# A pre-norm block pair with dense-evaluated expert layers: up-products of two experts interleaved, and pairs of heads and wider gate products in the second mixer

## The chip, the core and the metric

One core of a Trainium2 chip runs the whole program. The metric is the device time of one execution in microseconds. TensorE (PE) multiplies, its weight loads (PEld) run beside the multiplications; VectorE (DVE), ScalarE (ACT) and GpSimd (POOL) work on tiles, and SyncE (SP) issues most of the transfers.

## The reference

512 tokens of width 1024 pass through two blocks. The first mixes tokens with differential attention and retention, the second with a gated convolution and an mLSTM of eight heads; each is followed by the same kind of expert layer. What the change touches, cut to its core:

```python
# second mixer: i_pre, f_pre are 8 + 8 columns of the projection
proj = h @ w_in
ig = (i_pre + b_igate).transpose(0, 2, 1)
fg = (f_pre + b_fgate).transpose(0, 2, 1)
s_qk = einsum('bhtd,bhsd->bhts', qb, kb) * w_ts        # per head, d = 64
num = einsum('bhts,bhsv->bhtv', s_qk, vb) + ...        # v = 128

# expert layer: 128 * 128 = 16384 experts, 8 heads x 16 chosen per token
ub = take(u, eb);  z = einsum('thkd,td->thk', ub, hb)
a = gelu(z) * gb
out = einsum('thk,thkd->td', a, take(v, eb))
```

## The kernel before

All products that need fp32 accuracy are done as three in a rounded fp32 type: each operand is split into a high and a low part (ScalarE copies the high part, L86; VectorE subtracts for the low part, L87), and `mm3` (L99, its three matmuls are L101, L102 and L103) adds high x high, high x low and low x high into one PSUM accumulator.

The order is: first mixer (`mixer1`, L225), expert layer (`peer`, L447), second mixer (`mixer2`, L836), expert layer (`peer` again).

**The expert layer.** For three of the four token blocks (384 tokens) all 16384 experts are evaluated, in 128 groups of 128, each of which the code and this text call an expert e. `up(e)` (L495) loads a 128 x 1024 tile of weights through pool tag "w" (three buffers each of raw, high and low part), and issues 24 matmuls of 384 columns (8 blocks of the model width, three each) into a PSUM tile z of one bank, of which there are two; ScalarE applies gelu into a slot of a ring of 37 (L500). `down` (L681) multiplies the ring slot by the gate matrix wt (zero for experts that a token did not choose, VectorE L686), splits it into gh and gl, loads the expert's output weights through tag "v" (two buffers; expert 0 and part of the last ones use "w"), and issues 18 matmuls of 512 columns (L701) into six accumulators, three token blocks x two halves; consecutive matmuls go to the two halves in turn. wt is fetched for eight experts at a time from DRAM, where the router's work left it (L722). The first 36 up-products (LEAD) are done while the router still works; then the main loop (L725) goes on with one `up(e)` and one `down([e - 36])` per step, 92 steps with both. The last steps only have `down`, and the last two experts share one. The fourth token block's experts are gathered row by row (L708) and multiplied on VectorE (L711, L717) beside the main loop.

**The second mixer.** The normed input is written transposed, feature block by feature block, as fp32 (xf) and as split parts (L153 to L157). The 16 gate columns are computed in true fp32 with xf as the stationary operand: four token blocks x eight feature blocks of matmuls with 16 moving columns (L872), four copies (L873), eight transposes (L877) to get rows of the gates, two adds of the biases (L878). Then come the projections (L101 to L103 again), a chain on the gate rows (from L908), and a loop over the eight heads (L951): for each of four key blocks a decay row is fetched as a tile "we" (L957, four buffers), masked on GpSimd (L958) and exponentiated on ScalarE (L960); the scores of one head are an fp32 matmul over 64 rows (L962), VectorE multiplies both into "pw" (L965, six buffers); then ten matmuls of 129 columns per head give the weighted values (L973), which are normalised (L975 to L978).

A framework (tiles with pools) derives all waits from the buffers and orders each engine's instructions itself, so the order on an engine need not be that of the code.

## Time and profile before

| | us |
|---|---|
| median of three runs | 3453.27 (3444.09 to 3463.71) |
| profiled execution | 3443.86 |
| its span | 3442.0 |
| TensorE busy | 3328.5 (97%) |
| TensorE weight loads busy | 2889.2 (84%) |
| VectorE busy | 2496.2 (73%) |
| ScalarE busy | 1314.1 (38%) |
| GpSimd busy | 856.2 (25%) |

The mean granted clock of TensorE is 0.990 of full speed (full speed is 2.4 GHz, the other level 1.2 GHz). The profile gives busy time, and for each group of instructions what ended the idle time before it. A matmul's recorded duration is longer than its spacing, since matmuls overlap in the pipeline: the starts of neighbouring matmuls tell the rate. A matmul in true fp32 is recorded as two passes.

### The profile page before, as it was taken

To read this page: it belongs to the slowest core of one execution; us is meant where nothing else is said; L and a number is where in the kernel's file an instruction comes from. 1 tells how busy PE (TensorE), PEld (TensorE's weight loads), DVE (VectorE), ACT (ScalarE), POOL (GpSimd) and SP (SyncE) were. 2 spreads that over 40 slices of the span, in tenths; PEclk is the share of its full clock that TensorE was granted. 3 is DMA by queue.
4 is the path that set the end of the run, shared out by engine and by line. 5 is a ranking of instruction groups with operands and counts; after the bars stand their busy time and mean duration, and the time that the engine had idled before them with its cause. 6 is when DMAs were issued, how large, how long until landed. Compare 5 with 4: busy or idle time off the path is not lost. (4 is left out here: it accounts for less than half of the span.)

```text
span 3442.0 us, 46835 instructions
## 1 busy us (share of the span) xinstructions
PE 3328.5 (97%) x17462; PEld 2889.2 (84%) x17462; DVE 2496.2 (73%) x4641; ACT 1314.1 (38%) x1936; POOL 856.2 (25%) x732
## 2 busy tenths in 40 slices
PE   7989999899999999999999999899899999999998
PEld 6667889899999999777778888788899999999977
DVE  6765799777777787866565343779977777787785
ACT  4443345433333333334452223435533333333333
POOL 1000420144443444410000000240034444444420
PEclk9999999999999999999999999999999999999999
DMA  7212236799989888963437332325698899998883
GB/s 245 78 53 100 89 113 249 290 320 321 316 307 311 309 309 303 322 222 71 113 108 222 94 92 92 111 91 185 229 354 311 303 319 314 313 312 313 314 284 128
DMA packets 307396, 768.32 MB, mean 223 GB/s; under 512 B 22552, under 2 KB 123960, under 8 KB 300760
## 3 DMA queue, kind: packets, MB, share of 16 engines
q1 hardware_dynamic: 230832, 489.80, 42.6%
q0 software_dynamic: 76336, 275.53, 23.2%
q8 instruction: 136, 2.23, 0.3%
q14 instruction: 92, 0.75, 0.1%
HBM read 708.56 MB, written 56.69 MB: 222 GB/s over the span
## 5 line engine op out<-in xcount | busy, mean ns | idle before, releaser
L86 ACT ACTIVATE whi<-wraw 128x1024 fp32r<-128x1024 f32 x446 | 472.6, 1060 | 1109.8 <-PE z L102 547.8
L101 PE MATMUL z<-pxh,whi 128*128 128x384 f32 x2048 | 698.9, 341 | 3.8 <-ACT ga L500 2.5
L103 PE MATMUL z<-pxh,wlo 128*128 128x384 f32 x2048 | 695.5, 340 | 2.2 <-DVE wlo L87 2.2
L102 PE MATMUL z<-pxl,whi 128*128 128x384 f32 x2048 | 694.2, 339 | 0.8 <-DVE pxl L87 0.7
L87 DVE TENSOR_TENSOR wlo<-wraw,whi 128x1024 fp32r<-128x1024 f32 x398 | 485.1, 1220 | 284.5 <-ACT whi L86 284.3
L708 POOL DMA_INDIRECT row<-in_p_u,eidg x256 | 343.2, 1341 | 847.5 <-DVE row L711 466.4
L708 POOL DMA_INDIRECT row<-in_p_v,eidg x256 | 354.4, 1385 | 469.2 <-DVE yr L717 394.9
L717 DVE SCALAR_TENSOR_TENSOR yr<-row,gg,yr 128x1024 f32<-128x1024 f32 x254 | 325.8, 1283 | 144.5 <-DMA row<-in_p_v,eidg 141.7
L701 PE MATMUL acc<-vhi,gl 128*128 128x512 f32 x1308 | 406.2, 392 | 1.7 <-DVE gl L87 1.7
L701 PE MATMUL acc<-vhi,gh 128*128 128x512 f32 x1308 | 406.5, 392 | 0.1
L701 PE MATMUL acc<-vlo,gh 128*128 128x512 f32 x1308 | 405.3, 391 | 1.2 <-DVE vlo L87 1.2
L711 DVE SCALAR_TENSOR_TENSOR row<-row,pxr 128x1024 f32<-128x1024 f32 x256 | 309.0, 1222 | 122.3 <-DMA row<-in_p_u,eidg 121.4
L101 PEld LDWEIGHTS z<-pxh,whi 128*128 128x128 f32 x2048 | 384.8, 188 | 13.7 <-ACT ga L500 2.9
L102 PEld LDWEIGHTS z<-pxl,whi 128*128 128x128 f32 x2048 | 385.2, 188 | 11.9 <-DVE pxl L87 0.9
L103 PEld LDWEIGHTS z<-pxh,wlo 128*128 128x128 f32 x2048 | 384.8, 188 | 4.2 <-DVE wlo L87 3.9
L86 ACT ACTIVATE gh<-gw 128x384 fp32r<-128x384 f32 x256 | 134.5, 525 | 629.0 <-issue 383.1
L701 PEld LDWEIGHTS acc<-vlo,gh 128*128 128x128 f32 x1308 | 245.3, 188 | 56.3 <-DVE vlo L87 1.6
L701 PEld LDWEIGHTS acc<-vhi,gl 128*128 128x128 f32 x1308 | 245.2, 188 | 55.8 <-DVE gl L87 2.5
L701 PEld LDWEIGHTS acc<-vhi,gh 128*128 128x128 f32 x1308 | 243.7, 188 | 39.8 <-ACT gh L86 0.8
L87 DVE TENSOR_TENSOR vlo<-vraw,vhi 128x1024 fp32r<-128x1024 f32 x218 | 265.6, 1218 | 15.2 <-ACT vhi L86 15.2
L86 ACT ACTIVATE vhi<-vraw 128x1024 fp32r<-128x1024 f32 x218 | 230.7, 1058 | 42.0 <-DMA vraw<-in_p_v 34.1
L87 DVE TENSOR_TENSOR gl<-gw,gh 128x384 fp32r<-128x384 f32 x256 | 141.8, 554 | 136.2 <-ACT gh L86 135.7
(394 smaller groups left out, 5082.9 us busy)
## 6 DMA issues: line engine op xcount, KB each, us to landing
wraw<-in_p_uT SPq DMA_DIRECT2D x256, 512.0 KB, 5.6
vraw<-in_p_v SPq DMA_DIRECT2D x218, 512.0 KB, 5.7
wd<-wc SPq DMA_DIRECT2D x48, 1024.0 KB, 4.8
wt<-wd SPq DMA_DIRECT2D x32, 1536.0 KB, 13.0
wraw<-in_w_in SPq DMA_DIRECT2D x88, 512.0 KB, 4.6
adaw<-in_w_adaT SPq DMA_DIRECT2D x48, 512.0 KB, 4.5
wraw<-in_p_v SPq DMA_DIRECT2D x38, 512.0 KB, 5.3
wraw<-in_p_wq SPq DMA_DIRECT2D x32, 512.0 KB, 3.4
```

Of the source, the lines that this page charges most:

```text
L86: nc.scalar.activation(hi, src, AF.Copy)
L87: return (eng or nc.vector).tensor_tensor(lo, src, hi.bitcast(F32), op=ALU.subtract)
L101: mm(ps, lh, rh, start=start, stop=False)
L102: mm(ps, lh, rl, start=False, stop=False)
L103: mm(ps, ll, rh, start=False, stop=stop)
L701: nc.tensor.matmul(acc[j][n], gx[:, ts_], vx[:, n * 512:(n + 1) * 512], start=e == 0 and vx is vh and gx is gh, stop=e == P - 1 and gx is gl)
L708: nc.gpsimd.indirect_dma_start(out=row, out_offset=None, in_=lay["v" if half else "u"], in_offset=bass.IndirectOffsetOnAxis(ap=eidg[:, s:s ...
L711: nc.vector.scalar_tensor_tensor(row, row, 1.0, xr, op0=ALU.mult, op1=ALU.mult, accum_out=zg[:, s:s + 1])
L717: nc.vector.scalar_tensor_tensor(yr, row, gg[:, s:s + 1], yr, op0=ALU.mult, op1=ALU.add)
```

## The change

Three things. (1) A new `mm3s` issues the three products of `mm3` for several accumulators in turn, and a new `up2` uses it: the weights of two experts are loaded, and their 48 up-products alternate between the two z banks. The main loop calls it on every second step. (2) In the second mixer the gate columns become the stationary operand (16 columns) and xf the moving one (512 columns): eight matmuls into one 16 x 512 tile, one add of the bias, and two transfers to the two row tiles. (3) The scores of two heads, which lie in the two halves of the partitions, are issued in turn (`weighted`), with eight "pw" buffers for six; the value products follow for both heads.

```diff
--- before.py
+++ after.py
@@ -95,6 +95,13 @@
         nc.sync.dma_start(raw, view)
         self.last_split = self.split(hi, lo, raw, eng)
         return hi, lo
+
+    def mm3s(self, ops, start, stop):
+
+        mm = self.nc.tensor.matmul
+        for n in range(3):
+            for ps, lh, ll, rh, rl in ops:
+                mm(ps, ll if n == 2 else lh, rl if n == 1 else rh, start=start and n == 0, stop=stop and n == 2)
 
     def mm3(self, ps, lh, ll, rh, rl, start, stop):
         mm = self.nc.tensor.matmul
@@ -499,6 +506,15 @@
                 g.mm3(z, uh[:, k], ul[:, k], xh[:, k, S - TD:], xl[:, k, S - TD:], k == 0, k == KD - 1)
             nc.scalar.activation(ring[e % len(ring)], z, gelu)
 
+        def up2(e):
+
+            ws = [g.weights(lay["uT"][e + i], [P, KD, P]) for i in range(2)]
+            zs = [g.sb(zps, [P, TD], "z") for _ in range(2)]
+            for k in range(KD):
+                g.mm3s([(z, uh[:, k], ul[:, k], xh[:, k, S - TD:], xl[:, k, S - TD:]) for z, (uh, ul) in zip(zs, ws)], k == 0, k == KD - 1)
+            for i, z in enumerate(zs):
+                nc.scalar.activation(ring[(e + i) % len(ring)], z, gelu)
+
         def more(n, eng=None, keep=REST):
 
             nonlocal begun
@@ -723,8 +739,8 @@
             return wt
 
         for e in range(P + LEAD):
-            if begun <= e < P:
-                up(e)
+            if begun <= e < P and e % 2:
+                up2(e - 1)
             d = e - LEAD
             if d >= 0:
                 if d == 0:
@@ -848,9 +864,9 @@
         wcq = g.sb(sm, [P, 4, KD], "wcq")
         nc.gpsimd.dma_start(wca, a["conv_a_w"][0].rearrange("j (k p) -> p j k", p=P), allow_slow_non_contiguous=True)
         nc.gpsimd.dma_start(wcq, a["conv_qk_w"][0].rearrange("j (k p) -> p j k", p=P), allow_slow_non_contiguous=True)
-        big = g.sb(sm, [8, 2], "big")
-        nc.gpsimd.dma_start(big[:, 0:1], a["b_igate"][0].rearrange("(h o) -> h o", o=1))
-        nc.gpsimd.dma_start(big[:, 1:2], a["b_fgate"][0].rearrange("(h o) -> h o", o=1))
+        big = g.sb(sm, [16, 1], "big")
+        nc.gpsimd.dma_start(big[0:8], a["b_igate"][0].rearrange("(h o) -> h o", o=1))
+        nc.gpsimd.dma_start(big[8:16], a["b_fgate"][0].rearrange("(h o) -> h o", o=1))
         sc1 = g.sb(sm, [P, KD], "sc1")
         nc.vector.tensor_scalar(sc1, ada[:, KD:2 * KD], 1.0, None, op0=ALU.add)
         nc.vector.tensor_tensor(sc1, sc1, pre, op=ALU.mult)
@@ -865,17 +881,13 @@
             g.norm_to_fm(np_, psp, "ps", xh, xl, sc1, ada[:, 0:KD], f32=xf, xn=mix.rearrange("p k s -> p (k s)").rearrange("p (b d) -> p b d", b=NB))
             wif = g.sb(np_, [P, KD, 16], "wif")
             nc.gpsimd.dma_start(wif, w[:, 6144:6160].rearrange("(k p) c -> p k c", p=P))
-            gi = g.sb(np_, [P, NB, 16], "gi")
-            for b in range(NB):
-                ps = g.sb(psp, [P, 16], "ps")
-                for k in range(KD):
-                    nc.tensor.matmul(ps, xf[:, k, b * P:(b + 1) * P], wif[:, k], start=k == 0, stop=k == KD - 1)
-                nc.vector.tensor_copy(gi[:, b], ps)
-            for n, dst in ((0, irow), (1, frow)):
-                ps = g.sb(psp, [8, S], "ps")
-                for b in range(NB):
-                    nc.tensor.transpose(ps[:, b * P:(b + 1) * P], gi[:, b, n * 8:n * 8 + 8], g.ident)
-                nc.vector.tensor_scalar(dst, ps, big[:, n:n + 1], None, op0=ALU.add)
+            gi = g.sb(np_, [16, S], "gi")
+            ps = g.sb(psp, [16, S], "ps")
+            for k in range(KD):
+                nc.tensor.matmul(ps, wif[:, k], xf[:, k], start=k == 0, stop=k == KD - 1)
+            nc.vector.tensor_scalar(gi, ps, big, None, op0=ALU.add)
+            nc.sync.dma_start(irow, gi[0:8])
+            nc.sync.dma_start(frow, gi[8:16])
 
         def conv(dst, src, taps, wt, j):
             n = taps - 1
@@ -948,22 +960,35 @@
         nc.sync.dma_start(rd, R)
 
         hm = mix.rearrange("p k s -> p (k s)").rearrange("p (b h v) -> p b h v", b=NB, v=P)
-        for h in range(8):
-            ho = (h % 2) * 64
-            pw = []
+        pws = {}
+
+        def weighted(hp):
+
+            for h in (2 * hp, 2 * hp + 1):
+                pws[h] = []
             for sc in range(NB):
                 n = S - sc * P
-                e = g.sb(ml, [P, S], "we", bufs=4)
-                nc.sync.dma_start(e[:, :n], row_bc(rd[h, sc, sc * P:]))
-                nc.gpsimd.affine_select(out=e[:, :P], in_=e[:, :P], pattern=[[1, P]], compare_op=ALU.is_ge, fill=-1.0e30,
-                                        base=0, channel_multiplier=-1)
-                nc.scalar.activation(e[:, :n], e[:, :n], AF.Exp, bias=cols[:, 0, sc, h:h + 1])
-                qp = g.sb(psp, [P, S], "ps")
-                nc.tensor.matmul(qp[:, :n], qkT[ho:ho + 64, 4 + h // 2, sc * P:(sc + 1) * P], qkT[ho:ho + 64, h // 2, sc * P:],
-                                 start=True, stop=True)
-                p = g.sb(ml, [P, S], "pw", bufs=6)
-                nc.vector.scalar_tensor_tensor(p[:, :n], qp[:, :n], 0.125, e[:, :n], op0=ALU.mult, op1=ALU.mult)
-                pw.append(p)
+                qps = []
+                for i in range(2):
+                    qp = g.sb(psp, [P, S], "ps")
+                    nc.tensor.matmul(qp[:, :n], qkT[i * 64:i * 64 + 64, 4 + hp, sc * P:(sc + 1) * P], qkT[i * 64:i * 64 + 64, hp, sc * P:],
+                                     start=True, stop=True)
+                    qps.append(qp)
+                for i in range(2):
+                    h = 2 * hp + i
+                    e = g.sb(ml, [P, S], "we", bufs=4)
+                    nc.sync.dma_start(e[:, :n], row_bc(rd[h, sc, sc * P:]))
+                    nc.gpsimd.affine_select(out=e[:, :P], in_=e[:, :P], pattern=[[1, P]], compare_op=ALU.is_ge, fill=-1.0e30,
+                                            base=0, channel_multiplier=-1)
+                    nc.scalar.activation(e[:, :n], e[:, :n], AF.Exp, bias=cols[:, 0, sc, h:h + 1])
+                    p = g.sb(ml, [P, S], "pw", bufs=8)
+                    nc.vector.scalar_tensor_tensor(p[:, :n], qps[i][:, :n], 0.125, e[:, :n], op0=ALU.mult, op1=ALU.mult)
+                    pws[h].append(p)
+
+        for h in range(8):
+            if h % 2 == 0:
+                weighted(h // 2)
+            pw = pws.pop(h)
             for c2 in range(2):
                 po = g.sb(psp, [P, 2, P + 1], "ps")
                 for ci in range(2):
```

**The order on TensorE at the start of the main loop** (in the first expert layer; the second has the same pattern). z tiles are the accumulators of up-products, acc those of down-products; z_6309 before is expert 36, z_6373 expert 37; after, z_6347 and z_6348 are 36 and 37, and z_6259 is expert 35. Before, the last up-products of expert 36, the first expert's down-products (18, cut here), and what follows them:

```order
L101 MATMUL z_6309<-pxh_2297,whi_6304 128x384
L102 MATMUL z_6309<-pxl_2298,whi_6304 128x384
L103 MATMUL z_6309<-pxh_2297,wlo_6305 128x384
L701 MATMUL acc_1077_6294<-whi_6344,gh_6339 128x512
L701 MATMUL acc_1078_6295<-whi_6344,gh_6339 128x512
L701 MATMUL acc_1077_6294<-wlo_6345,gh_6339 128x512
```

```order
L701 MATMUL acc_1081_6298<-whi_6344,gl_6340 128x512
L701 MATMUL acc_1082_6299<-whi_6344,gl_6340 128x512
L101 MATMUL z_6373<-pxh_2297,whi_6368 128x384
L102 MATMUL z_6373<-pxl_2298,whi_6368 128x384
L103 MATMUL z_6373<-pxh_2297,wlo_6369 128x384
```

After the change:

```order
L109 MATMUL z_6259<-pxl_2298,whi_6254 128x384
L110 MATMUL z_6259<-pxh_2297,wlo_6255 128x384
L104 MATMUL z_6347<-pxh_2297,whi_6336 128x384
L717 MATMUL acc_1077_6294<-whi_6312,gh_6307 128x512
L717 MATMUL acc_1078_6295<-whi_6312,gh_6307 128x512
L717 MATMUL acc_1077_6294<-wlo_6313,gh_6307 128x512
```

```order
L717 MATMUL acc_1081_6298<-whi_6312,gl_6308 128x512
L717 MATMUL acc_1082_6299<-whi_6312,gl_6308 128x512
L104 MATMUL z_6348<-pxh_2297,whi_6342 128x384
L104 MATMUL z_6347<-pxl_2298,whi_6336 128x384
L104 MATMUL z_6348<-pxl_2298,whi_6342 128x384
L104 MATMUL z_6347<-pxh_2297,wlo_6337 128x384
```

Before, the 24 up-products of expert 36 stood whole ahead of the first 18 down-products; now one matmul of the pair 36/37 does, and the other 47 stand behind them.

**The order on TensorE at the gates of the second mixer**, from the last transposes of the norm on (wif is the gate weights, xf the normed input in fp32, fmh and fml its split parts). Before, its beginning and, after more of the same, its end:

```order
L135 MATMUL ps_14038<-ident,mix_2512_13949 128x128
L135 MATMUL ps_14039<-ident,mix_2512_13949 128x128
L872 MATMUL ps_14071<-wif_14068,xf_13975 128x16 x2
L872 MATMUL ps_14081<-wif_14068,xf_13975 128x16 x2
L872 MATMUL ps_14071<-wif_14068,xf_13975 128x16
```

```order
L872 MATMUL ps_14091<-wif_14068,xf_13975 128x16
L872 MATMUL ps_14101<-wif_14068,xf_13975 128x16
L877 MATMUL ps_14111<-ident,gi_14070 8x128
L877 MATMUL ps_14117<-ident,gi_14070 8x128
L877 MATMUL ps_14111<-ident,gi_14070 8x128 x3
L877 MATMUL ps_14117<-ident,gi_14070 8x128 x3
```

After the change:

```order
L142 MATMUL ps_14038<-ident,mix_2512_13949 128x128
L142 MATMUL ps_14039<-ident,mix_2512_13949 128x128
L887 MATMUL ps_14071<-xf_13975,wif_14068 16x512 x3
L108 MATMUL ps_14088<-fmh_13968,whi_14093 128x512
L109 MATMUL ps_14088<-fml_13969,whi_14093 128x512
L887 MATMUL ps_14071<-xf_13975,wif_14068 16x512 x2
L110 MATMUL ps_14088<-fmh_13968,wlo_14094 128x512
L887 MATMUL ps_14071<-xf_13975,wif_14068 16x512 x2
L108 MATMUL ps_14088<-fmh_13968,whi_14093 128x512
L887 MATMUL ps_14071<-xf_13975,wif_14068 16x512
L109 MATMUL ps_14088<-fml_13969,whi_14093 128x512
L110 MATMUL ps_14088<-fmh_13968,wlo_14094 128x512
```

The 32 narrow matmuls and the eight transposes are gone; eight wide matmuls stand in their place, from the third on with the first projection's matmuls between them.

**The order on TensorE in the head loop** (qkT are queries and keys, pw the weighted scores, va the values; ps tiles are PSUM). Before:

```order
L962 MATMUL ps_14773<-qkT_14127 128x512
L962 MATMUL ps_14783<-qkT_14127 128x384
L962 MATMUL ps_14793<-qkT_14127 128x256
L962 MATMUL ps_14803<-qkT_14127 128x128
L973 MATMUL ps_14807<-va_14448,pw_14775 128x129 x2
L973 MATMUL ps_14816<-va_14448,pw_14775 128x129
L973 MATMUL ps_14807<-va_14448,pw_14785 128x129
L973 MATMUL ps_14816<-va_14448,pw_14785 128x129
```

After the change:

```order
L974 MATMUL ps_14727<-qkT_14087 128x512
L974 MATMUL ps_14729<-qkT_14087 128x512
L974 MATMUL ps_14747<-qkT_14087 128x384
L974 MATMUL ps_14749<-qkT_14087 128x384
L974 MATMUL ps_14767<-qkT_14087 128x256
L974 MATMUL ps_14769<-qkT_14087 128x256
L974 MATMUL ps_14787<-qkT_14087 128x128
L974 MATMUL ps_14789<-qkT_14087 128x128
L998 MATMUL ps_14807<-va_14408,pw_14737 128x129 x2
L998 MATMUL ps_14807<-va_14408,pw_14757 128x129
```

Four scores and then the ten value products of a head (rows that show x2 are two) have become eight scores of two heads, the two heads in turn, and then the value products of both.

## Rows read from the trace of the kernel before

**Rows 1.** The page's shares of the span, first line.

```profile
PE 3328.5 (97%) x17462; PEld 2889.2 (84%) x17462; DVE 2496.2 (73%) x4641; ACT 1314.1 (38%) x1936; POOL 856.2 (25%) x732
```

**Rows 2.** A window in the main loop; columns: stretch, length, busy PE, PEld, DVE, ACT, POOL, clock, DMA.

```profile
700.00:800.00 100.00, 100.00 (x504) 91.06 (x503) 77.77 (x113) 35.57 (x48) 40.47 (x32) 1.00 0.93 322
```

**Rows 3.** TensorE's timeline of one expert: start, duration, instruction, count.

```profile
1007.46 0.35 PE L101 MATMUL z<-pxh,whi 128*128 128x384 f32 x1
...
1011.70 0.63 PE L701 MATMUL acc<-vhi,gh 128*128 128x512 f32 x2
...
1015.82 0.35 PE L101 MATMUL z<-pxh,whi 128*128 128x384 f32 x1
```

**Rows 4.** TensorE's timeline: down-products with either pool's weights, then projections.

```profile
1525.22 0.63 PE L701 MATMUL acc<-whi,gl 128*128 128x512 f32 x2
...
1528.02 0.63 PE L701 MATMUL acc<-whi,gl 128*128 128x512 f32 x2
...
1528.95 0.62 PE L701 MATMUL acc<-vlo,gh 128*128 128x512 f32 x2
...
1530.76 0.62 PE L701 MATMUL acc<-vhi,gl 128*128 128x512 f32 x2
...
1949.94 0.40 PE L101 MATMUL ps<-fmh,whi 128*128 128x512 f32 x1
...
1952.74 0.40 PE L101 MATMUL ps<-fmh,whi 128*128 128x512 f32 x1
```

**Rows 5.** Timelines of ScalarE and VectorE: the split of an expert's up-weights.

```profile
1011.72 1.06 ACT L86 ACTIVATE whi<-wraw 128x1024 fp32r<-128x1024 f32 x1 [2.95 <-PE z L102]
1014.39 1.22 DVE L87 TENSOR_TENSOR wlo<-wraw,whi 128x1024 fp32r<-128x1024 f32 x1
```

**Rows 6.** Timeline at the start of the first main loop.

```profile
646.96 0.38 SPq L722 DMA_DIRECT2D wt<-wd  x1
...
654.63 0.34 PE L101 MATMUL z<-pxh,whi 128*128 128x384 f32 x1
...
659.20 0.56 DVE L686 TENSOR_TENSOR gw<-x,wt 128x384 f32<-128x384 f32 x1 [6.45 <-DMA wt<-wd]
...
660.41 0.73 PE L701 MATMUL acc<-whi,gh 128*128 128x512 f32 x2 [1.39 <-ACT gh L86]
```

**Rows 7.** The same place in the second expert layer.

```profile
2512.41 0.56 DVE L686 TENSOR_TENSOR gw<-x,wt 128x384 f32<-128x384 f32 x1 [4.76 <-DMA wt<-wd]
...
2513.78 0.64 PE L701 MATMUL acc<-whi,gh 128*128 128x512 f32 x2
```

**Rows 8.** Timeline at the second mixer's gates, and a window there.

```profile
1598.12 12.31 PE L872 MATMUL ps<-wif,xf 128*128 128x16 f32 x62 [1.12 <-DVE xf L154]
...
1603.03 0.80 DVE L154 TENSOR_SCALAR xf<-ps,sc,ada 128x512 f32<-128x512 f32 x1
...
1611.79 0.78 PE L101 MATMUL ps<-fmh,whi 128*128 128x512 f32 x1
1600.00:1610.00 10.00, 10.00 (x48) 10.00 (x49) 5.38 (x10) 3.30 (x6) 0.00 (x0) 0.50 0.00 0
```

**Rows 9.** The head loop: timeline, SP's waits, transfers (KB each, us to landing).

```profile
1719.81 2.42 PE L962 MATMUL ps<-qkT 64*128 64x512 f32 x8
...
1721.39 1.16 DVE L965 SCALAR_TENSOR_TENSOR pw<-ps,we 128x512 f32<-128x512 f32 x2 [0.38 <-ACT we L960]
...
1726.79 0.69 DVE L965 SCALAR_TENSOR_TENSOR pw<-ps,we 128x512 f32<-128x512 f32 x1
...
1727.53 2.40 PE L973 MATMUL ps<-va,pw 128*128 128x129 f32 x18 [0.49 <-DVE pw L965]
SPq L957 <- DVE pw L965: 25.5, 14, 6.5
we<-rd SPq DMA_DIRECT2D x7, 256.0 KB, 3.4
```

**Rows 10.** TensorE's timeline in the first mixer: scores of two row halves in turn.

```profile
225.13 1.99 PE L391 MATMUL sc<-rqkT 64*128 64x512 f32 x8
```

## The prediction

> **What bounds the kernel now.** I read the page's shares first, then a table of windows, then single rows. By the shares TensorE is busy for 97% of the span of 3442.0 us [rows 1], so only 113.5 us of it are not matmul time. A window says where that time is not: in the main loop over the experts TensorE is busy for 100.00 of 100 us, issues 504 matmuls, and has a granted clock of 1.00 [rows 2]. So nothing that is only waited for can be won there; a matmul must become cheaper or there must be fewer of them. One expert takes 24 up-products from 1007.46 to 1011.70 (4.24 us, 176.7 ns each) and 18 down-products up to 1015.82 (4.12 us), 8.36 us in all [rows 3]. The places where TensorE is not at full rate are small: the start of each main loop, the gates of the second mixer, and its loop over heads. The change touches the loop body and all three places.
>
> The sum is made against the profiled execution, 3443.86 us, which is 0.27% below the median of the three runs, 3453.27; I add the sum to the median. A measurement of this kernel can tell about 0.5%, 17 us, from no change.
>
> **Up-products in pairs.** Per peer 92 experts go through the main loop's up-products, so 2 x 92 x 24 = 4416 matmuls change their neighbours: instead of 24 into one PSUM bank, 48 go to two banks in turn. Their number, columns and weight loads stay the same. What changes is whether the next matmul writes to the same bank. No row shows up-products in two banks, so I take the nearest rows. The down-products already alternate: twelve of 512 columns with weights from the same pool take 1525.22 to 1528.02, 2.80 us, 233.3 ns each. The projections put six in a row into one bank, and twelve of 512 columns take 1949.94 to 1952.74, also 2.80 us, 233.3 ns [rows 4]. Alternating and not alternating cost the same, so the gain per up-product is nothing. The bounds: the lowest rate for 512 columns in the trace is eight down-products in 1528.95 to 1530.76, 226.3 ns [rows 4], 13.0 ns above 512 columns at 2.4 GHz; 384 columns with that surplus are 173.0 ns, 3.7 ns below 176.7, times 4416 is -16 us. The other end is the same spread upwards (233.3 against 226.3, with other buffers read, scaled to 384 columns: +5 ns, +22 us). I take 0.
>
> The Trainium skill ("TensorE: Matmul & The Clock Gate", section on the back-to-back issue gap) gives N/2.4 + 2.5 ns for an isolated matmul at full clock, 162.5 ns for 384 columns. By that the sum would be up to 14 ns x 4416 = 62 us shorter if the same-bank order were what holds the rate up; the 233.3 ns of alternating rows, where the rule gives 215.8 ns, say that it is not.
>
> **Weights of two experts at once.** Pool "w" keeps three buffers. With two in use by a pair, the second expert of the next pair can be split only when the pair's last up-product is done. Then two groups of down-products follow, 2 x 4.12 = 8.24 us, before that split is needed. In the trace the same chain, released by the last up-product, goes: high part by ScalarE at 1011.72 (1.06 us), low part by VectorE from 1014.39 (1.22 us) to 1015.61 [rows 5], 3.9 us with a queue of 1.6 us on VectorE. 8.24 less 3.9 leaves 4.3 us; VectorE is busy for 78 of 100 us there [rows 2]. So I cost it at nothing; its cover are the 36 down-products, and every us by which the chain outlasts them costs 92 us (92 pairs).
>
> **The start of the main loop.** This is where I see a loss. The first down-products wait for gate weights: the transfer of wt is issued at 646.96, VectorE multiplies by it at 659.20 (after 6.45 us of waiting for that DMA), and 1.21 us later, behind ScalarE's split, the first down-product starts at 660.41. Meanwhile TensorE does the up-products of expert 36, from 654.63 for 24 x 0.1767 = 4.24 us, and waits for only 1.39 us [rows 6]. By the order of instructions after the change only one matmul of the pair 36/37 stands ahead of those 18 down-products, and 47 behind. The cover of 4.24 us shrinks to 0.18: +4.1 us, as nothing makes wt come earlier. In the second peer VectorE multiplies at 2512.41 and the down-product starts at 2513.78 without a wait [rows 7]; the multiply plus the 1.21 us of the first peer is 2513.62, so 0.16 us of slack is given up first: +3.9 us. Sum +8. Least: 0, if the transfer is issued earlier by as much, since its place in SP's queue may shift; most +14, if the longer idle time also costs clock, as in the stretch 1600 to 1610, where it was granted 0.50 [rows 8].
>
> **Gates of the second mixer.** Before: 64 recorded passes of 16 columns, the last 62 in 12.31 us from 1598.12, then eight transposes, the first projection at 1611.79 [rows 8]. They are late although their input is there: the last block of the normed input is written by 1603.83 (1603.03 + 0.80). After: eight matmuls of 512 columns in fp32, one per block. Price: the head loop's four fp32 matmuls of 512, 384, 256 and 128 columns take 2.42 us [rows 9], of which 512 columns are at most 512/1280 x 2.42 = 0.97 us. Eight are 7.7 us, and blocks come every 1.0 us, so the eighth ends by about 1604.8 (1603.83 + 0.97); projections stand between them in the new order. First undisturbed projection at 1604.8 for 1611.79: -7.0 us. Bounds: at the granted 0.50 of 1600 to 1610 [rows 8] each doubles, 8 x 1.94 = 15.5 from 1598.1, end 1613.6: +2. At best projections fill all gaps: -9.5. The two new transfers (gates to rows) feed only ScalarE's chain on the forget gate, and TensorE has the projections meanwhile: 0.
>
> **Head loop.** Two heads' scores now sit side by side in two halves of the array. That this runs at once is seen in the first mixer: eight passes (four matmuls of 512 columns, in row halves) in 1.99 us, for 4 x 0.97 = 3.9 alone [rows 10]. It would save 8 x 2.42 / 2 = 9.7 us of TensorE. But the loop does not wait for TensorE: SP waits for VectorE's last use of "we" 14 times, 25.5 us in all, there are still four "we" buffers, and the largest transfer takes 3.4 us [rows 9]. A turn of four buffers is 5.4 us, by the products at 1721.39 and 1726.79 [rows 9]: 3.4 us of transfer, 0.69 of product, the rest mask and exponential. There are eight turns before and after. After, every second turn has the short tiles (256 and 128 columns for 512 and 384; I estimate half of the 0.69 us, on ScalarE as on VectorE, hence 0.7 less): 4 x 0.7 = -3. Against it, at the end the value products of two heads (2.4 us each, [rows 9]) instead of one are left behind the last weighting: +2.4. Sum 0 (-0.6), bounds -9.7 and +5.
>
> **Sum.** 0 + 0 + 8 - 7 + 0 = +1 us; 3453 + 1 = **3454 us**.
>
> **Rivals.**
> 1. Alternation does pay: consecutive accumulation into one bank is what holds 176.7 ns above 160. For it: the down-products of the v pool, which alternate, are the fastest rows. Against: [rows 4], the same 233.3 ns. -16 us (173.0 ns) to -74 us (160 ns, no gap at all, 16.7 x 4416): 3438 to 3380. Chance 0.20, for more than 0.5% 0.15.
> 2. Slower: the second weights of a pair come late, once per pair. Place: VectorE's queue between the pair's last up-product and the next pair's second matmul. It decides once the chain takes more than 8.24 us, i.e. 4.3 us of VectorE or transfer time above [rows 5]; row products there wait for gathers, and may bunch. 0.5 us late is +46 us (3499), 1 us +92. Chance 0.12.
> 3. The head loop was bound by TensorE after all: -9.7 + 1, 3445. Against it: SP's 25.5 us of waiting. Chance 0.08 (0.03 for over 0.5%, with other gains).
> 4. Up-products become dearer by their operands' buffers (+5 ns, +22 us), or the starts lose clock: 3460 to 3480. Chance 0.07, half of it over 0.5%.
> 5. The clock. It is 1.00 in the loops although down-products change banks with each matmul [rows 2, 3]. If it fell to 0.9 over two loops of 92 x 8.36 = 769 us, the price would be 1538 x 0.11 = +170 us, 3620. The Trainium skill (same page, section on a second failure mode of the clock gate) says that cycling through PSUM banks on each iteration made the engine pause often enough for its clock to swing; by that rule the change would be harmful, and the trace disagrees, as the alternating down-products show no idle time. Chance 0.03.
>
> **How the numbers follow.** My forecast keeps 0.50. Faster: 0.15 + 0.03 = 0.18. Slower: 0.12 + 0.03 + 0.04 = 0.19. Same: 0.63. The range reaches down to the floor of 173.0 ns with the gate's best (-16 - 3 - 3 = -22, 3432) and up to the dearer up-products with the starts' wait (+22 + 4 = +26, 3480); beyond lie the larger cases of rivals 1, 2 and 5, about 2 in 10.
>
> **What would show it.** Windows at 700 to 1400: 504 matmuls per 100 us again, TensorE at 100.00; 48 up-products in 8.5 us. More than 506 speaks for rival 1; idle time before an up-product, put down to wlo or whi, for rival 2. At about 655 one up-product, then 5 to 6 us of idle time to the first down-product, released by ScalarE's gh or VectorE's gl, and the same once near 2510. The first undisturbed projection 13 us or less behind the first transposes' end. In the head loop shorter scores on TensorE and the same waits of SP. I am wrong if an up-product's spacing moves by more than 4 ns or any wait occurs once per pair.

## The result and the profile after

The changed kernel takes 3498.97 us (median of four runs, 3492.58 to 3503.13), the kernel before on the same chip 3448.68 us: a ratio of 1.0145, 95% interval 1.0124 to 1.0167. That is 50 us slower; the forecast was no difference that can be told.

The page's shares of the changed kernel, its whole span and the first line of section 1:

```profile
span 3494.6 us, 46797 instructions
PE 3340.2 (96%) x17406; PEld 2885.3 (83%) x17406; DVE 2482.2 (71%) x4636; ACT 1300.7 (37%) x1936; POOL 855.1 (24%) x732
```

Against [rows 1] no engine is busy for longer except TensorE, by 11.7 us; the rest of the 52.6 us of span is idle time of TensorE, 113.5 us before and 154.4 now. Where it lies is seen in a long window of each main loop (columns as in [rows 2]). Before:

```profile
700.00:1400.00 700.00, 700.00 (x3518) 637.58 (x3517) 541.66 (x670) 247.25 (x335) 297.89 (x218) 1.00 0.90 312
2560.00:3260.00 700.00, 700.00 (x3515) 637.36 (x3514) 546.08 (x671) 248.41 (x336) 302.01 (x218) 1.00 0.91 314
```

After:

```profile
700.00:1400.00 700.00, 683.79 (x3418) 619.16 (x3417) 524.55 (x661) 232.35 (x324) 286.46 (x211) 1.00 0.88 304
2560.00:3260.00 700.00, 690.21 (x3449) 626.10 (x3448) 525.30 (x666) 237.46 (x332) 294.11 (x213) 1.00 0.88 306
```

TensorE was busy without a gap; now it idles for 16.2 and 9.8 us of the 700 and does 100 and 66 matmuls less. The list of TensorE's waits over the whole program (total us, times, longest) begins with a wait for the low part of up-weights, wlo, that the kernel before hardly has. Before, and after:

```profile
PE z L103 <- DVE wlo L87: 2.2, 3, 0.7
```

```profile
PE z L104 <- DVE wlo L87: 29.5, 31, 3.0
```

All 31 stand at the sixth matmul of a pair, the first that needs the second expert's low part; 92 pairs went by, so a third of them waited.

One of the 31, on TensorE's timeline, and the instructions of VectorE and then ScalarE ahead of it:

```profile
1061.51 0.53 PE L104 MATMUL z<-pxh,whi 128*128 128x384 f32 x2
1061.87 0.51 PE L104 MATMUL z<-pxl,whi 128*128 128x384 f32 x2
1062.22 0.34 PE L104 MATMUL z<-pxh,wlo 128*128 128x384 f32 x1
1064.45 0.44 PE L104 MATMUL z<-pxh,wlo 128*128 128x384 f32 x1 [1.89 <-DVE wlo L87]
```

```profile
1055.56 1.23 DVE L727 SCALAR_TENSOR_TENSOR row<-row,pxr 128x1024 f32<-128x1024 f32 x1 [1.02 <-DMA row<-in_p_u,eidg]
1056.71 0.08 DVE L727 DVE_READ_ACCUMULATOR row<-row,pxr 128x1 f32 x1
1062.03 1.23 DVE L727 SCALAR_TENSOR_TENSOR row<-row,pxr 128x1024 f32<-128x1024 f32 x1 [5.23 <-DMA row<-in_p_u,eidg]
1063.18 0.08 DVE L727 DVE_READ_ACCUMULATOR row<-row,pxr 128x1 f32 x1
1063.18 2.36 DVE L87 TENSOR_TENSOR wlo<-wraw,whi 128x1024 fp32r<-128x1024 f32 x2
```

```profile
1052.97 1.06 ACT L86 ACTIVATE whi<-wraw 128x1024 fp32r<-128x1024 f32 x1 [3.61 <-PE z L104]
1054.68 1.06 ACT L86 ACTIVATE whi<-wraw 128x1024 fp32r<-128x1024 f32 x1
```

The pair before ended at 1052.97; that frees the buffer for the second expert of this pair, whose high part is made at once, from 1052.97 to 1054.03 (the other high part belongs to the pair after). Its low part is the first of the two at 1063.18: in VectorE's order it stands behind a gathered row product for which VectorE idles for 5.23 us until the transfer lands. This pair starts at 1061.51 and needs that low part with its sixth matmul; there TensorE loses 1.89 us. The order of instructions on VectorE shows that two low parts stand together so in every pair but the first few of each loop. Before the change, and after it (names without numbers; `row,zg<-row,pxr` is a row product; in the second half of a loop they are `yr<-row,gg,yr`):

```
before                      after
L87  wlo<-wraw,whi          L87  wlo<-wraw,whi   second of the next pair
L87  gl<-gw,gh              L87  wlo<-wraw,whi   first of the pair after it
L686 gw<-x,wt               L87  gl<-gw,gh
L87  vlo<-vraw,vhi          L702 gw<-x,wt
L711 row,zg<-row,pxr        L87  vlo<-vraw,vhi
L711 row,zg<-row,pxr        L727 row,zg<-row,pxr
L87  wlo<-wraw,whi          L727 row,zg<-row,pxr
L87  gl<-gw,gh              L727 row,zg<-row,pxr
L686 gw<-x,wt               L87  gl<-gw,gh
L87  vlo<-vraw,vhi          L87  vlo<-vraw,vhi
L711 row,zg<-row,pxr        L727 row,zg<-row,pxr
L711 row,zg<-row,pxr        L702 gw<-x,wt
L711 row,zg<-row,pxr        L727 row,zg<-row,pxr
```

Row products stood right ahead of a low part before as well, but two or three between it and the one before; now two low parts come together, with five or six row products since the last two. There are three tiles for gathered rows, and GpSimd issues a gather only when a row product has freed one, so of five row products in a run the last have their gathers issued during the run. VectorE waits longer for the gathers than before; the page's rows for the row products of a loop's first half, before and after:

```profile
L711 DVE SCALAR_TENSOR_TENSOR row<-row,pxr 128x1024 f32<-128x1024 f32 x256 | 309.0, 1222 | 122.3 <-DMA row<-in_p_u,eidg 121.4
```

```profile
L727 DVE SCALAR_TENSOR_TENSOR row<-row,pxr 128x1024 f32<-128x1024 f32 x256 | 308.0, 1222 | 201.4 <-DMA row<-in_p_u,eidg 201.2
```

What makes this count is the lead. Before, the buffer that an expert's last up-product frees is used three experts later, so a low part had 3 x 8.36 - 4.24 = 20.8 us from the release to its use. Now the second expert's is used in the very next pair, 8.24 us and five matmuls (0.9 us) later.

The other places. Start of the second main loop, TensorE's timeline and VectorE's multiply:

```profile
2537.15 0.33 PE L104 MATMUL z<-pxh,whi 128*128 128x384 f32 x1
2542.43 1.22 PE L717 MATMUL acc<-whi,gh 128*128 128x512 f32 x2 [4.95 <-ACT gh L86]
```

```profile
2541.21 0.56 DVE L702 TENSOR_TENSOR gw<-x,wt 128x384 f32<-128x384 f32 x1 [5.96 <-DMA wt<-wd]
```

One up-product and then 4.95 us of waiting, where there was none [rows 7]. Behind it two down-products take 1.22 us instead of 0.64, at a granted clock of 0.51 (columns as in [rows 2], then GB/s):

```profile
2541.90:2545.30 3.40, 2.87 (x7) 2.29 (x8) 2.69 (x4) 3.40 (x6) 0.00 (x0) 0.51 1.02 406
```

In the first expert layer it waited for 1.91 us instead of 1.39 [rows 6], with the clock at 0.50 behind it as well (664.60 to 668.00): there the up-products of expert 35 themselves ended 7 us later, as TensorE came to the layer later.

The gates, TensorE's timeline:

```profile
1629.96 3.04 PE L887 MATMUL ps<-xf,wif 128*16 128x512 f32 x6
1632.93 0.50 PE L108 MATMUL ps<-fmh,whi 128*128 128x512 f32 x1
...
1633.60 1.89 PE L887 MATMUL ps<-xf,wif 128*16 128x512 f32 x4
...
1635.85 1.89 PE L887 MATMUL ps<-xf,wif 128*16 128x512 f32 x4
...
1638.10 1.03 PE L887 MATMUL ps<-xf,wif 128*16 128x512 f32 x2
1639.06 0.51 PE L109 MATMUL ps<-fml,whi 128*128 128x512 f32 x1
```

From the first of the eight wide matmuls (two records each) to the first undisturbed projection it is 9.1 us; in [rows 8] it was 13.7 from the third record on. TensorE is busy throughout in both, but at a granted clock of 0.50 there and of 0.97 here, although the transposes just before (1626.00 to 1629.90) had 0.50 here too:

```profile
1630.00:1640.00 10.00, 10.00 (x25) 2.66 (x25) 8.36 (x13) 5.90 (x10) 0.00 (x0) 0.97 0.00 0
```

The head loop, TensorE's timeline of one pair's scores, and SP's waits:

```profile
1739.43 2.43 PE L974 MATMUL ps<-qkT 64*128 64x512 f32 x16
```

```profile
SPq L980 <- DVE pw L985: 27.9, 13, 6.5
```

A table of stretches between the starts of TensorE's instructions, in us, from the timelines of the two profiled executions:

| stretch | before | after | difference |
|---|---|---|---|
| start to first down-product | 660.41 | 663.98 | +3.6 |
| to the last up-product of the first main loop | 760.75 | 789.57 | +28.8 |
| to the first gate matmul | 175.44 | 176.41 | +1.0 |
| to the first score of the head loop | 106.26 | 98.73 | -7.5 |
| to the last value product | 46.01 | 47.69 | +1.7 |
| to the first down-product of the second layer | 764.90 | 766.05 | +1.2 |
| to the last up-product | 761.88 | 781.45 | +19.6 |
| to the end | 166.36 | 170.70 | +4.3 |

The main loops' stretches hold 23 more up-products now, because these moved behind the first down-product (23 x 0.176 = 4.0 us); so 24.8 and 15.5 us are lost inside them, and the stretch ahead of each should have become 4.0 us shorter. Counted from start to start, the matmuls that waited account for 21.9 and 13.1 us of the loss. Most of the rest is lost by matmuls at the lower clock, at the start and once inside each loop: behind the wait of 2.0 us that ended at 806.5 the granted clock fell to 0.50 for 3.4 us, and likewise behind the longest, 3.0 us up to 3212.9. The first (columns as in [rows 2], then GB/s):

```profile
808.00:811.40 3.40, 3.40 (x13) 3.39 (x12) 3.37 (x6) 1.47 (x2) 0.62 (x2) 0.50 0.84 264
```

The +3.6 us of the first row needs a caution: up to the first main loop TensorE has the same instructions in the same order, and the eight profiles of the experiments reach the first up-product at 318 to 322 us, this one at 323, the one of before at 316.49. So up to 6.8 us of the 52.6 between these two executions are scatter of that kind; the medians differ by 50. The last row is scatter too as far as can be seen: from the last up-product to the end it is 165.5 to 173.1 us in the seven other profiles that keep the gathers.

### The profile page after: what moved, and what is told of

Read it like the earlier page. It is cut to its first block, busy times and chain, and to the rows that moved or that the text cites. A ratio compares the mean times of both kernels' runs of the same rounds, so it can differ in the third digit from the quotient of the medians.

```text
span 3494.6 us, 46797 instructions
## 1 busy us (share of the span) xinstructions
PE 3340.2 (96%) x17406; PEld 2885.3 (83%) x17406; DVE 2482.2 (71%) x4636; ACT 1300.7 (37%) x1936; POOL 855.1 (24%) x732
## 3 DMA queue, kind: packets, MB, share of 16 engines
q1 hardware_dynamic: 230864, 489.84, 42.2%
## 4 chain that ended last, share of the span: by engine, by line
PE 31%; issue 17%; DMA 17%; DVE 13%; POOL 6%; ACT 1%; POOLq 0%; DVEq 0%; SPq 0%; ACTq 0%
DMA row<-in_p_v,eidg 13%; PE acc L717 9%; POOL row L724 6%; PE ps L108 6%; PE ps L110 6%; PE ps L109 6%; PE z L104 3%; DMA row<-in_p_u,eidg 3%; DVE wlo L87 2%; DVE yr L733 1%; DVE oh L669 1%; DVE o L667 1%; DVE o L670 1%; DVE row L727 1%; DVE o L668 1%
## 5 line engine op out<-in xcount | busy, mean ns | idle before, releaser
L104 PE MATMUL z<-pxh,wlo 128*128 128x384 f32 x1472 | 390.2, 342 | 29.8 <-DVE wlo L87 29.5
L104 PE MATMUL z<-pxh,whi 128*128 128x384 f32 x1472 | 380.7, 339 | 0.0
L104 PE MATMUL z<-pxl,whi 128*128 128x384 f32 x1472 | 379.9, 339 | 0.0
L104 PEld LDWEIGHTS z<-pxh,wlo 128*128 128x128 f32 x1472 | 269.1, 188 | 42.0 <-DVE wlo L87 41.9
L104 PEld LDWEIGHTS z<-pxh,whi 128*128 128x128 f32 x1472 | 269.8, 188 | 7.8
L104 PEld LDWEIGHTS z<-pxl,whi 128*128 128x128 f32 x1472 | 268.9, 188 | 0.1
L108 PE MATMUL z<-pxh,whi 128*128 128x384 f32 x576 | 201.4, 350 | 1.9 <-ACT ga L507 1.0
```

The costliest lines, as they stand in the source:

```text
L104: mm(ps, ll if n == 2 else lh, rl if n == 1 else rh, start=start and n == 0, stop=stop and n == 2)
L108: mm(ps, lh, rh, start=start, stop=False)
```

## The experiments

The theories. **A**: the low parts come late because they stand together on VectorE behind row products that wait for their gathers (of the two that stand together only the first is due; the expectations speak of both as one pair's, which the rows above correct). **B**: they come late because three weight buffers let the second split begin only when the pair ends. **C**: the loss comes from the gates or the heads. For the heads, **D**: the four "we" buffers bound the loop; **E**: TensorE does.

**The pairs of up-products alone** (`e1_up2_only`): the kernel before with `mm3s`, `up2` and the changed call, and nothing else.

> Theory A (VectorE's order: the low parts of a pair's two up-weights stand together at the end of its queue, behind about five gathered row products that wait for their transfers) and theory B (the third weight buffer: the second split is released only by the pair's last up-product) both expect the whole loss here: the gates' gain of about 7 us is given back too, so 3500 to 3507 us, with about 30 us of TensorE's idle time put down to wlo. Theory C (the loss comes from the gates or the heads, which shift what follows) expects within 10 us of the kernel before, 3440 to 3460.

3501.6 us, ratio 1.0139 (1.0109 to 1.0169). TensorE's waits:

```profile
PE z L104 <- DVE wlo L87: 26.7, 29, 2.6
```

The loss is in the pairs; C falls.

**No gathers** (`e2_no_gather`), on the changed kernel; the fourth block's rows are not fetched, and its products use a tile that is there, so that part of the output is another:

```diff
-            nc.gpsimd.indirect_dma_start(out=row, ...
-                nc.vector.scalar_tensor_tensor(row, row, 1.0, xr, ...
+                nc.vector.scalar_tensor_tensor(row, xr, 1.0, xr, ...
-                nc.vector.scalar_tensor_tensor(yr, row, gg[:, s:s + 1], yr, ...
+                nc.vector.scalar_tensor_tensor(yr, xr, gg[:, s:s + 1], yr, ...
```

> The gathers of the fourth token block's expert rows are left out; VectorE does the same row products on a tile that is there. So VectorE's work and order stay, and only the waits for transfers go (with their traffic). Theory A: the idle time put down to wlo falls from 29.5 us to under 4 us, the main loops take 92 x 8.36 = 769 us again, 3448 to 3458 us in all. Theory B: the splits are still released by the pair's end, the idle time stays near 30 us and the time above 3485.

3422.69 us, ratio 0.9913 (0.9884 to 0.9942), below the range that was given. The windows of the main loops:

```profile
700.00:1400.00 700.00, 700.00 (x3530) 639.09 (x3529) 544.96 (x677) 244.15 (x337) 0.00 (x0) 1.00 0.48 151
2560.00:3260.00 700.00, 700.00 (x3525) 639.12 (x3524) 543.42 (x665) 243.05 (x336) 0.00 (x0) 1.00 0.48 149
```

VectorE does as much as ever (545 us of 700) with the same three weight buffers, and TensorE has no gap. From the start of an expert's high part to the end of its low part it is 2.3 us throughout. So it is not VectorE's work that is too much, but its idling for a transfer while a low part stands behind. (The traffic goes too, DMA share 0.48 for 0.88; the next run keeps it.) What was missed: without gathers the ends of both layers, where only down-products and rows are left, get shorter too (last up-product to last down-product 153.2 and 153.7 us, in the kernel before 165.1 and 157.2), and TensorE waits for the gates' high part at the two starts for 1.1 us in all, instead of 6.9.

**Another order, with the buffers, gathers and traffic kept** (`e3_order_fix`), on the changed kernel. Two things change at once, the place of the row products and the step in which a pair's weights are asked for:

```diff
+        def load2(e):
+            return [g.weights(lay["uT"][e + i], [P, KD, P]) for i in range(2)]
...
-            if begun <= e < P and e % 2:
-                up2(e - 1)
+            if begun <= e < P:
+                if e % 2:
+                    up2(e - 1, ws)
+                else:
+                    ws = load2(e)
+                    wl = g.last_split
...
-                with tc.issue_after(g.last_split.ins):
+                with tc.issue_after(g.last_split.ins), tc.issue_after(wl.ins):
```

The row products of a step are queued on VectorE behind the second low part of the pair whose loads were asked for last.

> The pair's weights are asked for one step earlier, and the row products of a step are queued on VectorE behind both low parts of the next pair, so one low part has gl and vlo ahead of it alone and the other two row products at most. Buffers, gathers and traffic as after the change. Theory A: idle time put down to wlo under 10 us, 3455 to 3470 us. Theory B: about 30 us of it and 3490 to 3500. If a low part that is placed early holds up gl behind it, idle time before the down-products grows instead.

3458.77 us, ratio to the kernel before 1.0032 (1.0015 to 1.0049): 40 of the 50 us are back. The windows:

```profile
700.00:1400.00 700.00, 700.00 (x3529) 639.06 (x3529) 534.36 (x678) 241.28 (x336) 283.58 (x219) 1.00 0.91 314
2560.00:3260.00 700.00, 700.00 (x3524) 638.91 (x3523) 536.54 (x675) 243.25 (x337) 286.36 (x219) 1.00 0.91 315
```

Same gathers, same buffers, full traffic, no gap. The second expert's low part, the one that is due, ends 3.5 and 3.0 us on average after its high part began (first and second loop), 5.8 at most; in the changed kernel it was 9.3 and 8.5, 12.6 at most. The order is not quite the one expected, as up to four row products stand between two low parts, but they stand ahead of the one that is not due. Theory A stands, and B as a cause by itself falls by both runs: the split still begins when the pair ends, and nothing waits. The short lead that the three buffers leave is needed for the loss all the same; a fourth weight buffer, and more tiles for gathered rows, were not tried. What is left is the start, where a new wait is seen, twice in all (each layer once):

```profile
665.25 0.47 ACT L507 ACTIVATE ga<-z 128x384 f32<-128x384 f32 x1
665.78 0.69 PE L104 MATMUL z<-pxh,whi 128*128 128x384 f32 x1 [5.19 <-ACT ga L507]
```

With the pair 36/37 ahead of the first down-products the second expert needs the z bank of expert 35, whose gelu stands on ScalarE behind the split that waits for wt. So the wait for wt reaches TensorE by another way.

**That, and expert 36 alone at the start** (`e6_order_single`): pairs 37/38 to 125/126, the first and the last expert alone.

> As the run with the row products queued behind the low parts, but expert 36 is done alone ahead of the first down-products, as before the change, then pairs 37/38 to 125/126, then 127 alone. If one matmul of cover for wt is what costs the 5.0 us in the second layer's start (1.9 in the first), that idle time goes, 3450 to 3455 us; the loops take 769 us each. If the order of the row products matters by itself, which turns by one step here, low parts are late again and the time is 3465 or more.

3453.35 us, ratio 1.0031 (1.0016 to 1.0046). The start of the second layer:

```profile
2516.11 0.73 PE L720 MATMUL acc<-whi,gh 128*128 128x512 f32 x2 [0.89 <-ACT gh L86]
```

0.89 us for 4.95: the cover works as costed. But the order on VectorE turned by one step. In the first loop other parts are late now, and it takes 769.6 us for 760.8 in the kernel before (the second 762.1 for 761.9). TensorE's waits from 660 to 1440 us, its start included, are for the low part of the down-weights and the gates' high part:

```profile
PE acc L720 <- DVE vlo L87: 4.9, 5, 1.7
PE acc L720 <- ACT gh L86: 3.3, 4, 1.2
```

The ratio is that of the run before it, so what the start gave back was lost again. No order of pairs that was tried is faster than the kernel before.

**The gates alone** (`e4_gates_only`): the kernel before with the wide gate matmuls.

> The kernel before with the wide gate matmuls alone. From the first gate matmul to the first score of the head loop 106.3 us before and 98.7 after; so 98 to 99.5 here, and 6 to 9 us less in all: 3439 to 3443. If the gain there is given back in what follows (the first splits of the projections' weights, which wait for a transfer), 3446 to 3450.

3441.94 us, ratio 0.9984 (0.9968 to 1.0001). From the first gate matmul to the first score 98.57 us, as expected; the total fell by the 6 us expected, but the interval reaches 1, so the runs alone do not tell it. The stretch does: it is 98.5 to 98.8 us in all seven profiles with the wide gates and 105.7 to 106.3 in the three without.

**The pairs of heads alone** (`e5_heads_only`).

> The kernel before with the pairs of heads alone. Theory D (the loop waits for the four we buffers, so TensorE's cheaper scores gain nothing): the loop, 46.0 us before and 47.7 in the changed kernel, takes 46 to 49; 3446 to 3452 us in all. Theory E (TensorE bound it): 36 to 40 us, 3438 to 3442.

3445.44 us, ratio 0.9998 (0.9983 to 1.0013); the loop takes 46.4 us, in D's range, and SP still waits for VectorE's last use of "we":

```profile
SPq L968 <- DVE pw L973: 26.5, 15, 6.5
```

So D, and not E, for the loop with four "we" buffers.

**More "we" buffers, heads one by one** (`e7_gates_we3`) and **in pairs** (`e8_gates_heads_we3`), both with the wide gates:

```diff
-                e = g.sb(ml, [P, S], "we", bufs=4)
+                e = g.sb(ml, [P, n], f"we{sc}", bufs=3)
-                p = g.sb(ml, [P, S], "pw", bufs=6)
+                p = g.sb(ml, [P, n], f"pw{sc}", bufs=2)
```

> The wide gates alone, heads one by one as before, but three we buffers for each of the four sizes instead of four of the largest (and two pw for each size instead of six). Theory D: the waits of the transfer queue for we go, TensorE bounds the loop with 8 x 4.9 = 39 us, 40 to 42 with its start instead of 47.2: 3434 to 3437 us. Theory E: 46 to 47 us, 3441 to 3443.

3439.82 us, ratio 0.9979 (0.9964 to 0.9995), above D's range and below E's; in the total it can't be told from the gates alone. The loop takes 42.2 us instead of 47.2 with the gates alone, TensorE is busy for 40.9 of them, and it waits there for 1.3 us only. What was missed: SP's waits did not go, they fell from 27.1 to 19.7 us.

```profile
PE ps L969 <- DVE pw L961: 1.3, 2, 0.9
```

```profile
SPq L953 <- DVE pw L961: 19.7, 11, 6.5
```

> The wide gates, pairs of heads, and three we and two pw buffers for each size. Theory D: now the scores' 9.7 us can be gained too; the next bound is ScalarE (2.2 us of exponentials a head, with the normalising some 3) and the pairs' chain: 32 to 38 us, 3428 to 3434 us, the fastest kernel of all. Theory E: 37 to 40 us.

3432.39 us, ratio 0.9965 (0.9951 to 0.9978), the fastest here of the kernels with the same output, by the medians 14 us below the kernel before on its chip. The loop takes 39.5 us, outside D's 32 to 38 and inside E's 37 to 40. TensorE does not bound it, though: it is busy for 33.4 us of the loop. Its scores of a pair still come late, now because their accumulators wait for the weighting of the tiles before, and SP waits for that too.

```profile
PE ps L958 <- DVE pw L969: 3.1, 2, 1.6
PE ps L982 <- DVE pw L969: 2.5, 5, 0.9
```

```profile
SPq L964 <- DVE pw L969: 21.3, 9, 6.5
```

Whether more accumulators or more "pw" tiles would shorten it was not tried. The 2.6 us to the run before come from one profile each, and the loop in pairs with four "we" buffers took 46.2 to 49.2 us in five profiles, so by the loops alone the gain of the pairs is not shown; the medians of the totals are 7 us apart, and the two intervals overlap.

## Why the prediction was wrong

The step that failed is "Weights of two experts at once", where I cost the split chain at nothing, with 4.3 us to spare. Its frame was right: the second expert's split is released by the pair's last up-product and has the 36 down-products, 8.24 us, as cover. What was wrong is the chain's length, 3.9 us. It came from one instance, [rows 5], in which VectorE did not idle for a gather while the low part stood behind it. Another instance in the same trace of before, four experts later, is more than twice as long; ScalarE's high part, then VectorE:

```profile
1045.16 1.06 ACT L86 ACTIVATE whi<-wraw 128x1024 fp32r<-128x1024 f32 x1 [2.95 <-PE z L102]
```

```profile
1045.45 1.23 DVE L711 SCALAR_TENSOR_TENSOR row<-row,pxr 128x1024 f32<-128x1024 f32 x1 [1.92 <-DMA row<-in_p_u,eidg]
...
1048.79 1.23 DVE L711 SCALAR_TENSOR_TENSOR row<-row,pxr 128x1024 f32<-128x1024 f32 x1 [2.10 <-DMA row<-in_p_u,eidg]
...
1051.35 1.22 DVE L711 SCALAR_TENSOR_TENSOR row<-row,pxr 128x1024 f32<-128x1024 f32 x1 [1.32 <-DMA row<-in_p_u,eidg]
...
1052.50 1.22 DVE L87 TENSOR_TENSOR wlo<-wraw,whi 128x1024 fp32r<-128x1024 f32 x1
```

From 1045.16 to 1053.72 it is 8.6 us, with three row products ahead that waited for their gathers, and it cost nothing only because there were 20.8 us for it.

Over the experts of the main loops before, the chain (start of the high part to end of the low part) took 6.3 us on average in the first layer, and in 20 of 89 cases counted more than the 8.24 us of cover; in the second it took 4.6 us, and never more than 8.2. So in the first layer the long chain was there to be read before the change. In the second it was not: there the new order on VectorE, which I did not read, made it long. Afterwards, in the instance above, it is from 1052.97 to about 1064.4, 11.4 us; the low parts that are due took 9.3 and 8.5 us on average, and half of them (42 of 87) more than the 9.1 us that there are. Both changed, then: the cover, as costed, and the chain, which was taken to stay at 3.9.

Rival 2 had the mechanism, the place (rows that wait for gathers and bunch) and a price that came out: it gave 3499 us for half a us late per pair. The measured mean is (24.8 + 15.5) / 92 = 0.44 us, but 0.5 was an example and not worked out, so that it came so close is luck: two thirds of the pairs do not wait, the others for up to 3.0 us. It got a chance of 0.12. VectorE's busy share, 78%, was the wrong number to lean on: it does not show how long VectorE idles with work queued behind, and the run without gathers shows the same work in the same windows with no stall.

The other steps, in turn:

- **Up-products in pairs**: 0 was taken, and it is so. Over the two long windows an up-product starts 176.5 ns after the one before in the changed kernel and in the two runs without gaps, and 176.7 before (steps over 0.26 us left out): 0.2 ns, or under 1 us over 4416. In the runs without gaps 3529 matmuls go into 700 us for 3518, 0.3% more, but most of that is the down-products', 228.0 ns for 229.3. In a group of down-products the first nine steps average 231 ns, the last takes 235 and the others 226.7, and a group has 36 now for 18. Rival 1 falls. So does, for this stream, the isolated gap of 162.5 ns that the Trainium skill ("TensorE: Matmul & The Clock Gate", section on the back-to-back issue gap) would have given.
- **The start of the main loop**: +8 was forecast for both layers. The second shows 4.95 us of waiting (3.9 forecast); the first 0.5 us more only (4.1 forecast), since TensorE happened to arrive later. Behind both the granted clock was 0.50 for 3.4 us, and from start to start the down-products there lost some 1.5 us in each. That is 8.5 us in all, so the total is right in part by luck: the first layer's wait was smaller than forecast, and the clock, which stood only in the upper bound, made up for it.
- **Gates**: -7.0 was forecast; -7.5 us to the first score, and 98.57 for 106.26 us when the change is made alone. The records of a wide matmul start 0.43 us apart, 0.87 us for its two (0.97 was the price), and the clock, 0.50 there in [rows 8], was 0.97.
- **Head loop**: 0 was forecast; +1.7 us in the changed kernel, +0.4 alone, and with the same loop 46.2 and 49.2 us in two other profiles, so none of this is clear of scatter. Scores did become half as long on TensorE (2.43 us for 16 passes, for 2.42 us for eight in [rows 9]), and SP's waits stayed, as forecast; rival 3 falls.
- **The clock**: 1.00 as the mean of both long windows, although now up-products change banks as well; it fell to 0.50 once in each loop, each time behind a wait for a low part. In the run with the other order, which changes banks as often and has no gap, it did not fall in the windows. The observation of the Trainium skill ("TensorE: Matmul & The Clock Gate", section on a second failure mode of the clock gate) that cycling through PSUM banks made the engine pause often enough for its clock to swing is not borne out here; the gaps come from a late operand.

With the low parts in time, in the run with the other order, the change costs 11 us against the kernel before on its chip, for +1 in the sum. The two starts alone have 10.2 us of waiting there, where the sum had +8. That 3454 is close to that run's 3458.77 says less: the kernel before had 3453.27 where the sum began and 3447.82 there.

## What to carry to other kernels

When work is grouped, read the new order on the engine that prepares the operands, not only on the one that uses them: an engine that works in order and must idle for a transfer can have no slack to lend at a busy share of 78%. Two operands that used to be needed one after the other have to be ready at the earlier of the two times, and their buffers are freed later; look at what stands ahead of the second in the new order, take its chain from the longest instance and not from one that happens to be short, and queue work that waits for gathers behind it. Before a bound engine's instruction is made cheaper, find which buffer releases the loop: half-price scores gained nothing with four "we" tiles, and more "we" tiles gained 5 us of the loop with the scores at full price.

## What the runs showed of the hardware

Changing the bank with each of the 384-column matmuls costs nothing and gives nothing (176.5 ns for 176.7). A change between 384-column and 512-column matmuls has its price: in a group of 512-column matmuls the first nine steps average 231 ns, the last takes 235, the others 226.7. The granted clock fell to 0.50 for 3.4 us behind waits of 2.0 and 3.0 us inside the loops, where TensorE had been busy before, but not behind another of 2.0 us (at 1116.7). A gathered transfer was waited for by up to 5.23 us on VectorE in the changed kernel, and with no gathers at all the same work on VectorE fitted. The 16-column gate products took 12.31 us for 62 passes, at a granted clock of 0.50 from 1600 us on [rows 8] with TensorE busy throughout; the same sums as eight wide matmuls took 7.9 us (3.04 + 1.89 + 1.89 + 1.03) with projections in between, in a stretch with a clock of 0.97.
